# Differential attention written by hand as rows of names: the group norm's matmul placed behind a value or key product, and the first output projection product placed one row earlier where the heads end

## Chip, cores and metric

The program runs on one core of a Trainium2 chip. The metric is the time of one execution in microseconds (us) as the device reports it; of several executions the median counts. A separate execution was recorded by the hardware profiler, and all quoted rows come from it. TensorE is PE in the profile (its weight loads are PEld), VectorE is DVE, ScalarE is ACT, GpSimd is POOL, and SyncE, which issues most DMAs, is SP.

## What is computed

The program is a two-layer encoder trunk on 1024 tokens of width 1024. Layer 0 mixes tokens by differential attention and layer 1 by latent attention; each is followed by a gated MLP with a short convolution. The change touches only layer 0's attention and the start of its output projection:

```python
def block(args):
    qb, blk = args
    sc = jnp.einsum('bqhcd,bkhcd->bhcqk', qb, k).astype(jnp.float32) * scale
    p = masked_softmax(sc, chunk_mask(blk, s)[None, None, None])
    a = p[:, :, 0] - lam * p[:, :, 1]
    return jnp.einsum('bhqk,bkhe->bqhe', a.astype(v.dtype), v)
...
o = from_blocks(lax.map(block, (to_blocks(q), jnp.arange(nb))))
o = rms_norm(o, subln_g) * (1.0 - lambda_init)
return o.reshape(b, s, D_MODEL) @ w_o
```

There are 8 heads, each with two score maps (c = 0 and 1). The softmax of the second, times a scalar, is subtracted from the first; the result weighs the values; each head's output is RMS-normalised over its 128 columns (the group norm) and goes through the output projection.

## The kernel before

Every product of float32 operands is made of three matmuls of high and low parts (`mm3`, lines 119 to 121): high by low, high by high, low by high. So each operand must first be split into a rounded high part (ACT, `hi`, line 127) and the remainder (DVE or POOL, `lo`, line 130).

Attention is cut into 32 steps: step 4h + p is head h with the query pair p, that is 256 query rows against the keys up to there. A step is an object (`DaStep`) with small named parts, and a unit of projection work (queries, keys or values of 512 tokens) has named parts too. `da_steps` (line 346) walks through rows t = -1 to 34. A row is a string of names; a name without a mark belongs to step t, with one `'` to step t - 1, with two to step t - 2, with `+` to step t + 1. Names of steps that don't exist are passed over. The rows are taken from `DA_SCORE[t % 4]`, with `DA_SECOND` for t = 1 and the seven rows of `DA_END` for t = 28 to 34. Within these rows the order on PE, DVE, ACT and POOL is exactly that of the names (`manual_schedule`); SP's DMAs are placed by the framework's own scheduler.

The names that matter here:

- `S0`, `S1` are the scores of the two query blocks (lines 1871 and 1872), `M` their row maxima (DVE, line 1886 or 1882), `E` the exponentials (ACT, line 1897), `I` the reciprocals of the sums, `C` the scaling of the first map, `X0`, `X1` the subtraction of the second map (DVE, line 1910).
- `T` turns a piece of the weights on PE (line 1918), `H` and `L` split it (ACT, DVE), `A` multiplies it by the values on PE, `O` copies the result out (ACT).
- `Q1`, `Q2`, `Q3` square the output for the group norm: two on ACT (lines 1952, 1955), `Q3` on POOL, the remainder (line 130). `F` sums the squares over the columns with two matmuls by ones (lines 1963, 1964). `R1`, `R2`, `R3` on ACT (lines 1970, 1972, 1974) and `N1`, `N2`, `N3` on DVE (1979, 1981, 1983) make the inverse root and store the head's output.
- `U0`, `U1` are the first and second half (12 matmuls each) of a projection product, `V0`, `V1` those of the row's second unit. Both accumulate in the one PSUM bank with the tag `u`. For queries and keys the bank is read out by `Us` and `Um` on DVE (lines 601 and 605); `Ua`, `Up` go on on POOL; `Uqa` to `Uqf` split the queries on ACT and POOL.
- In the last rows `d`, `b`, `c` load and split the output projection's weights (`c3` on DVE), `g0` issues the loads for output tile 0, `h0` (ACT) and `l0` (POOL) split its input, `Y0` and `Z0` are the two halves of its product, 12 matmuls each into the bank `u`, and `y0`, `z0` add them to the residual (DVE, line 746).

PSUM has eight banks: three with the tag `b` (turned pieces, outputs, the norm's sums), one `u`, and two pairs `S`. In rows with p of 2 or 3 each `S0` or `S1` takes both `S` pairs, one for each score map, so `S1` writes where `S0`'s scores were, after `E0a` and `E0b` have read them.

Of the kernel before, what the change touches and what calls it, by code (L numbers as in the profile page):

```python
# [56 lines left out]
class Trunk:  # L57
# [234 lines left out]
    def steps(self, attend, units, prepare, n, apart=False):  # L292
# [33 lines left out]

    DA_SCORE = (
# [4 lines left out]
    )  # L332

    DA_SECOND = "S0 I1' Vc' H2'' M0 Ukd' L2'' A1'' C0' X0' H3'' E0b L3'' U0 E0a A2'' Wh Vt' N3'''' A3'' O'' Wl' Q2'' C1' I0 X1' U1 C0 S1 X0 Us Vh' Q1'' T0' H0' Q3'' Up F'' Um M1 Ua Wl R1'' Vl' E1b V0 E1a L0' I1 A0' Uqa R2'' R3'' Uqd Uqb C1 N1'' Uqe X1 Uqc V1 T1 T0 Uqf H0"

    DA_END = (
# [9 lines left out]
    def da_steps(self, attend, units, prepare, n, extra):  # L346
# [4 lines left out]
        with self.tc.manual_schedule(engines={E.PE, E.DVE, E.Activation, E.Pool}):  # L351
            for t in range(-1, first + len(self.DA_END)):
                while len(steps) < min(n, t + 2):
# [3 lines left out]
                    for name, u in zip("UV", units(x)):  # L357
                        steps[x].parts.update({name + part: f for part, f in u.items()})
                row = self.DA_SECOND if t == 1 else self.DA_SCORE[t % 4] if t < first else self.DA_END[t - first]
                for name in row.split():  # L360
# [1961 lines left out]
```

## Time and profile before

| what | value |
|---|---|
| median of 3 runs | 2386.11 us (2383.92 to 2387.11) |
| span of the profiled execution | 2381.6 us |
| runs' median less that span | 4.5 us |
| PE busy | 2344.1 us, 98% |
| DVE busy | 1931.5 us, 81% |
| ACT busy | 1288.2 us, 54% |
| POOL busy | 613.7 us, 26% |
| first and last of the 16 group norm sums (`F`, line 1963) | start at 92.6 and 496.9 us |

The profiled execution's own time beside its span is not among the three times; the table gives the distance between the span and the median of the runs instead. A row of the timeline has the start in us from the span's start, the duration, the engine, the line in the kernel, the operation, the tiles written and read, the shape, and how many equal ones were merged; in brackets stands how long the engine was idle before it and what ended that. Matmuls overlap in the pipeline: one of 512 columns lasts 0.39 us, but the next starts about 0.23 us later, so distances between starts are what counts. A row of the view of waits has the waiting instruction, the one waited for, the sum in us, how often, and the longest.

### The profile page before, as it was taken

What the parts mean: (1) busy time and instruction counts of PE and PEld (TensorE: products, weight loads), DVE (VectorE), ACT (ScalarE), POOL (GpSimd) and SP (SyncE); (2) the same over time, 40 slices, a digit from 0 to 9 for tenths busy, and PEclk for the clock granted to TensorE, in tenths of its full rate; (3) what the DMA queues carried; (4) which work ended last, traced back from release to release, by engine and by line L of the source; (5) the groups of instructions that cost most, each with busy time, mean ns of one, the idle gap of its engine ahead of it and who ended that gap; (6) DMA issues with size and microseconds to landing.
All of it is one profiled execution on the core that took longest, in us unless ns stands there. A gap on an engine that the chain in (4) does not pass through costs nothing.

```text
span 2381.6 us, 32686 instructions
## 1 busy us (share of the span) xinstructions
PE 2344.1 (98%) x11954; PEld 1994.6 (84%) x11954; DVE 1931.5 (81%) x3185; ACT 1288.2 (54%) x2365; POOL 613.7 (26%) x486
## 2 busy tenths in 40 slices
PE   8999999999999999999999999999999999999998
PEld 7888888888888888888898889988888888887886
DVE  6788888858888888899865888886588888888997
ACT  6777677735444444354444778775354444443544
POOL 4555555324000000000133666673320000000001
PEclk9999999999999999999999999999999999999999
DMA  3111111332222222652222211133322222227502
GB/s 147 41 36 37 49 36 54 115 111 102 94 83 80 80 89 80 230 167 94 82 97 58 72 32 39 41 98 105 117 74 93 80 80 82 87 80 282 177 1 80
DMA packets 95664, 213.39 MB, mean 90 GB/s; under 512 B 8712, under 2 KB 33936, under 8 KB 95504
## 3 DMA queue, kind: packets, MB, share of 16 engines
q1 hardware_dynamic: 86304, 183.51, 23.3%
q10 hardware_dynamic: 9200, 27.80, 3.2%
q8 instruction: 94, 1.54, 0.3%
q14 instruction: 66, 0.54, 0.1%
HBM read 158.85 MB, written 52.43 MB: 89 GB/s over the span
## 4 chain that ended last, share of the span: by engine, by line
PE 86%; DVE 6%; DMA 2%; POOL 2%; issue 2%; ACT 1%; SPq 0%; POOLq 0%; DVEq 0%; ACTq 0%
PE S L119 13%; PE S L121 13%; PE S L120 13%; PE b L119 8%; PE b L121 8%; PE b L120 8%; PE u L119 4%; PE u L121 4%; PE u L120 4%; PE b L263 2%; PE u L2028 2%; PE u L2027 1%; PE S L1872 1%; PE S L1871 1%; PE b L1918 1%
## 5 line engine op out<-in xcount | busy, mean ns | idle before, releaser
L167 POOL TENSOR_TENSOR st<-st,mhalf 128x1 f32<-128x1 f32 x56 | 35.8, 641 | 1294.3 <-DVE st L164 1286.6
L119 PE MATMUL S<-s,u 128*128 128x512 f32 (+1 forms) x800 | 302.4, 378 | 1.9 <-DVE s L130 1.9
L121 PE MATMUL S<-s,u 128*128 128x512 f32 (+1 forms) x800 | 301.6, 377 | 1.5 <-DVE u L130 0.8
L120 PE MATMUL S<-s,u 128*128 128x512 f32 (+1 forms) x800 | 301.3, 377 | 0.0
L127 ACT CAST u<-h 128x512 fp32r<-128x512 f32 (+2 forms) x242 | 145.6, 619 | 275.2 <-DVE h L1026 271.9
L119 PE MATMUL b<-s,u 128*128 128x512 f32 x588 | 231.0, 393 | 1.1 <-DVE u L130 0.4
L121 PE MATMUL b<-s,u 128*128 128x512 f32 x588 | 229.3, 390 | 0.0
L120 PE MATMUL b<-s,u 128*128 128x512 f32 x588 | 229.2, 390 | 0.0
L1083 DVE SCALAR_TENSOR_TENSOR u<-u,conv,u 128x1023 f32<-128x1023 f32 (+1 forms) x176 | 224.8, 1277 | 0.8 <-ACT u L1079 0.7
L149 POOL TENSOR_TENSOR u<-u,st 128x512 f32<-128x512 f32 (+7 forms) x160 | 172.2, 1085 | 168.5 <-DVE st L2013 106.7
L127 ACT CAST s<-u 128x512 fp32r<-128x512 f32 (+3 forms) x229 | 144.4, 664 | 93.7 <-PE u L121 26.4
L119 PEld LDWEIGHTS S<-s,u 128*128 128x128 f32 x800 | 150.5, 188 | 30.1 <-DVE s L130 2.6
L130 DVE TENSOR_TENSOR u<-b,u 128x512 fp32r<-128x512 f32 (+1 forms) x256 | 158.5, 631 | 21.2 <-ACT u L127 19.1
L121 PEld LDWEIGHTS S<-s,u 128*128 128x128 f32 x800 | 150.6, 188 | 29.3 <-DVE u L130 1.0
L120 PEld LDWEIGHTS S<-s,u 128*128 128x128 f32 x800 | 150.6, 188 | 27.3
L127 ACT CAST u<-b 128x512 fp32r<-128x512 f32 (+1 forms) x256 | 134.6, 547 | 71.0 <-PE b L1918 40.8
L119 PE MATMUL u<-s,s 128*128 128x512 f32 (+1 forms) x408 | 162.7, 399 | 1.6 <-DVE s L130 0.9
L121 PE MATMUL u<-s,s 128*128 128x512 f32 (+1 forms) x408 | 158.1, 388 | 0.0
L120 PE MATMUL u<-s,s 128*128 128x512 f32 (+1 forms) x408 | 157.8, 387 | 0.0
L1086 ACT ACTIVATE u<-u 128x1024 f32<-128x1024 f32 x44 | 46.7, 1062 | 187.4 <-DVE u L1083 187.4
L130 DVE TENSOR_TENSOR s<-u,s 128x512 fp32r<-128x512 f32 (+2 forms) x204 | 139.1, 715 | 10.6 <-ACT s L127 10.3
L130 DVE TENSOR_TENSOR u<-h,u 128x512 fp32r<-128x512 f32 x171 | 117.4, 687 | 32.6 <-ACT u L127 31.5
(294 smaller groups left out, 6518.4 us busy)
## 6 DMA issues: line engine op xcount, KB each, us to landing
u<-in_ffn_up SPq DMA_DIRECT2D x88, 512.0 KB, 3.8
g_d<-u ACTq DMA_DIRECT2D x44, 512.0 KB, 2.6
u<-in_ffn_down SPq DMA_DIRECT2D x66, 256.0 KB, 5.2
u<-g_d SPq DMA_DIRECT2D x62, 256.0 KB, 4.2
s<-in_da_wqkv SPq DMA_DIRECT2D x23, 512.0 KB, 3.6
x_d<-u SPq DMA_DIRECT2D x16, 512.0 KB, 2.9
s<-x_d SPq DMA_DIRECT2D x8, 1024.0 KB, 9.9
u<-o_d SPq DMA_DIRECT2D x24, 256.0 KB, 3.1
```

The lines of the kernel that those rows point to most:

```text
L119: mm(out, lh, rl, start=first, stop=False, skip_group_check=onto)
L120: mm(out, lh, rh, start=False, stop=False, skip_group_check=onto)
L121: mm(out, ll, rh, start=False, stop=last, skip_group_check=onto)
L127: self.nc.scalar.copy(out, src)
L130: (eng or self.nc.vector).tensor_sub(out, src, hi.bitcast(F32))
L149: self.nc.gpsimd.tensor_mul(x, x, s.to_broadcast(list(x.shape)))
L167: nc.gpsimd.tensor_tensor(r, s, self.mhalf, ALU.pow)
L263: self.nc.tensor.transpose(ps[:, j * P : (j + 1) * P], probs[t][:, k : k + P], self.ident)
L1083: nc.vector.scalar_tensor_tensor(t[half][:, back:], u[half][:, : S - back], w, t[half][:, back:], ALU.mult, ALU.add)
L1086: nc.scalar.activation(t[0], t[0], AF.Silu)
L1871: nc.tensor.matmul(sc[c][:, b : b + m], ql[c][:, qs], kt[:, c, :m], start=True, stop=False)
L2028: nc.tensor.matmul(o[:, c0:], v, ah, start=False, stop=kb == 2 * p + 1)
```

## The change

Four rows of names are written anew; no part is added or taken away.

In the second row of `DA_SCORE` (rows 5, 9, 13, 17, 21, 25) `F''` stands behind `V0` instead of ahead of `Um`, and `R1''` stands next to `R2''`. The row for t = 1 has the same edit, but there `F''` and `R1''` belong to step -1, which doesn't exist. In `DA_END`, `g0` and `c3` move up within row 29, and `h0`, `l0` and `Y0` come up from row 30 into row 29:

```diff
-        "S0 I1' Vc' H2'' M0 Ukd' L2'' A1'' C0' X0' H3'' E0b L3'' U0 E0a A2'' Wh Vt' N3'''' A3'' O'' Wl' Q2'' C1' I0 X1' U1 C0 S1 X0 Us Vh' Wl Q1'' T0' H0' Q3'' Up F'' Um M1 Ua R1'' Vl' E1b V0 E1a L0' I1 A0' Uqa R2'' R3'' Uqd Uqb C1 N1'' Uqe X1 Uqc V1 T1 T0 Uqf H0",
+        "S0 I1' Vc' H2'' M0 Ukd' L2'' A1'' C0' X0' H3'' E0b L3'' U0 E0a A2'' Wh Vt' N3'''' A3'' O'' Wl' Q2'' C1' I0 X1' U1 C0 S1 X0 Us Vh' Wl Q1'' T0' H0' Q3'' Up Um M1 Ua Vl' E1b V0 F'' E1a L0' I1 A0' Uqa R1'' R2'' R3'' Uqd Uqb C1 N1'' Uqe X1 Uqc V1 T1 T0 Uqf H0",
...
-        "S0 M0 A1'' Up Ukc' b3 E0a L3'' Ua A2'' X0' A3'' Uqa Ukd' Uqc I1 O'' X1' Q1'' Q2'' Q3'' Uqb Uqd T0' H0' Uqf F'' E0b L0' Uqe g0 c3",
-        "S0 h0 M0a I0' l0 C1' C0' R1''' E0a R2''' M0b g1 A0'' Y0 E0b X1' X0' S1 R3''' h1 g2 T0' N1''' O'' y0 M1b N2''' Vt'' H0' T1' E1b Z0 M1a Vh'' E1a L0' z0 H1' l1 Vl'' L1'",
+        "S0 M0 A1'' Up Ukc' b3 E0a L3'' Ua g0 A2'' X0' A3'' Uqa Ukd' Uqc I1 O'' h0 X1' c3 Q1'' Q2'' l0 Q3'' Uqb Uqd T0' Y0 H0' Uqf F'' E0b L0' Uqe",
+        "S0 M0a I0' C1' C0' R1''' E0a R2''' M0b g1 A0'' E0b X1' X0' S1 R3''' h1 g2 T0' N1''' O'' y0 M1b N2''' Vt'' H0' T1' E1b Z0 M1a Vh'' E1a L0' z0 H1' l1 Vl'' L1'",
```

What this does to the order on PE in row 5 (rows 9, 13, 17, 21 and 25 are alike), before: `T0'` turns into `b_1304`, `F''` sums into `b_1313`, and `V0` starts in the bank `u_1329`, followed by `A0'` into `b_1346`.

```order
L1918 MATMUL b_1304<-ident,u_228_1140 128x128
L1918 MATMUL b_1304<-ident,u_234_1159 128x128 x2
L1963 MATMUL b_1313<-h_257_1310,ones 128x512
L1964 MATMUL b_1313<-h_250_1271,ones 128x512
L119 MATMUL u_1329<-s_51_148,s_212_1070 128x512
...
L119 MATMUL b_1346<-u_256_1308,u_213_1074 128x256
```

And with the change, where the names' numbers are others but the parts the same (`u_1323` is `V0`'s bank, `b_1336` the sum, `b_1343` the output):

```order
L1918 MATMUL b_1304<-ident,u_228_1140 128x128
L1918 MATMUL b_1304<-ident,u_234_1159 128x128 x2
L119 MATMUL u_1323<-s_51_148,s_212_1070 128x512
...
L1963 MATMUL b_1336<-h_257_1310,ones 128x512
L1964 MATMUL b_1336<-h_250_1271,ones 128x512
L119 MATMUL b_1343<-u_256_1308,u_213_1074 128x256
```

The two matmuls by ones moved behind `V0`'s twelve matmuls, so that these now stand directly behind the turning.

On ACT in the same row the piece of the difference is this (line 1970 is `R1''`, lines 1972 and 1974 `R2''` and `R3''`, line 1897 `E1b` and `E1a`, the casts to `u` are the query splits):

```order
-L1970 ACTIVATE h_262_1323<-b_1313,eps 128x512
-L1897 ACTIVATE u_264_1327,st_263_1326<-S_1290,st_260_1318 128x512 x2
-L127 CAST u_267_1353<-h_259_1316 64x512
-L1972 ACTIVATE h_261_1322<-h_262_1323 128x512
-L1974 ACTIVATE h_262_1323<-h_261_1322 128x512
-L127 CAST u_267_1353<-h_259_1316 64x512 x3
+L1897 ACTIVATE u_261_1321,st_260_1320<-S_1290,st_259_1315 128x512 x2
+L127 CAST u_265_1350<-h_258_1313 64x512
+L1970 ACTIVATE h_267_1353<-b_1336,eps 128x512
+L1972 ACTIVATE h_266_1352<-h_267_1353 128x512
+L1974 ACTIVATE h_267_1353<-h_266_1352 128x512
+L127 CAST u_265_1350<-h_258_1313 64x512 x3
```

`R1''` moved from ahead of the two exponentials to right ahead of `R2''`; on DVE the order of this row is unchanged.

At the end of the heads, PE in rows 29 and 30 before: `T0'` into `b_4749`, `F''` into `b_4756`, `S0` into `S_4766` and `S_4767`, `A0''` into `b_4797`, `Y0` into `u_4804`, then `S1` into `S_4821` and `S_4822`.

```order
L1918 MATMUL b_4749<-ident,u_861_4596 128x128 x2
L1963 MATMUL b_4756<-h_890_4745,ones 128x512
L1964 MATMUL b_4756<-h_889_4743,ones 128x512
L1871 MATMUL S_4766<-u_809_4316,h_59_156 128x512
...
L119 MATMUL b_4797<-u_892_4753,u_842_4502 128x256
...
L119 MATMUL u_4804<-s_856_4570,u_897_4776 128x512
...
L1871 MATMUL S_4821<-u_809_4316,h_59_156 128x512
```

And with the change (`b_4756` is now the turned piece, `u_4760` is `Y0`, `b_4776` the sum, `S_4782` `S0`'s scores, `b_4810` `A0''`):

```order
L1918 MATMUL b_4756<-ident,u_861_4596 128x128 x2
L119 MATMUL u_4760<-s_856_4570,u_889_4743 128x512
...
L1963 MATMUL b_4776<-h_892_4752,ones 128x512
L1964 MATMUL b_4776<-h_891_4749,ones 128x512
L1871 MATMUL S_4782<-u_809_4316,h_59_156 128x512
...
L119 MATMUL b_4810<-u_895_4773,u_842_4502 128x256
...
L1871 MATMUL S_4821<-u_809_4316,h_59_156 128x512
```

`Y0`'s twelve matmuls left the place between `S0` and `S1` of row 30 and stand ahead of `F''` and `S0`. On ACT `h0` now precedes `Q1''`, on POOL `l0` precedes `Q3''`, and on DVE `c3` precedes `L0'`; the order of SP's DMAs is the same as before.

More of the change, by code (lines that the diff above doesn't have):

```diff
@@ L332 @@
     )
-    DA_SECOND = "S0 I1' Vc' H2'' M0 Ukd' L2'' A1'' C0' X0' H3'' E0b L3'' U0 E0a A2'' Wh Vt' N3'''' A3'' O'' Wl' Q2'' C1' I0 X1' U1 C0 S1 X0 Us Vh' Q1'' T0' H0' Q3'' Up F'' Um M1 Ua Wl R1'' Vl' E1b V0 E1a L0' I1 A0' Uqa R2'' R3'' Uqd Uqb C1 N1'' Uqe X1 Uqc V1 T1 T0 Uqf H0"
+    DA_SECOND = "S0 I1' Vc' H2'' M0 Ukd' L2'' A1'' C0' X0' H3'' E0b L3'' U0 E0a A2'' Wh Vt' N3'''' A3'' O'' Wl' Q2'' C1' I0 X1' U1 C0 S1 X0 Us Vh' Q1'' T0' H0' Q3'' Up Um M1 Ua Wl Vl' E1b V0 F'' E1a L0' I1 A0' Uqa R1'' R2'' R3'' Uqd Uqb C1 N1'' Uqe X1 Uqc V1 T1 T0 Uqf H0"
     DA_END = (
         "O'' d0 Up X1' S1 S0 V0 R2''' Ua R3''' M1 d1 b0 b1 M0 c0 T0' V1 E1b N1''' T2' H0' L0' E1a c1 Uka +S1 d2 Vc E0a N2''' b2 Ukb E0b N3''' T1' +U0 T3' H2' H1' +M1 I1 +U1 I0 c2 +E1b +E1a L2' L1' d3 +Us A0' +Um C1 C0 H3'",
[2 rows of a table removed]
[2 rows of a table added]
         "S0 I1' A0'' h2 C1' I0' A1'' Y1 C0' O'' M0a X1' X0' y1 g3 T0' Q1'' M0b E0a T2' H0' N3'''' T1' H1' E0b L0' I0 l2 C0 Z1 Q2'' L1' z1 H2' h3",
```

## The prediction

> **What bounds the kernel.** I read the page's first part, then the view of waits with PE as the waiting engine over 60 to 760 us, then the timeline of PE at the waits that the change addresses.
>
> ```profile
> span 2381.6 us, 32686 instructions
> PE 2344.1 (98%) x11954; PEld 1994.6 (84%) x11954; DVE 1931.5 (81%) x3185; ACT 1288.2 (54%) x2365; POOL 613.7 (26%) x486
> PE b L1963 <- POOL h L130: 3.1, 7, 0.8
> ```
>
> PE is busy for 98% of the span, so what isn't a wait of PE, or doesn't become one, costs nothing. The change moves no matmul out of the program. It can gain only from idle PE: `F''` (line 1963) waits seven times for `Q3''` on POOL, 3.1 us in all; six of these are rows 5 to 25, the seventh and longest is row 29.
>
> **Part 1: `F''` behind `V0`, six times.** Row 9 stands for all; its PE, DVE and ACT rows:
>
> ```profile
> 167.50 0.49 PE L1918 MATMUL b<-ident,u 128*128 128x128 f32 x3
> 168.37 0.50 PE L1963 MATMUL b<-h,ones 128*128 128x512 f32 x1 [0.38 <-POOL h L130]
> 168.70 0.40 PE L1964 MATMUL b<-h,ones 128*128 128x512 f32 x1
> 168.94 0.39 PE L119 MATMUL u<-s,s 128*128 128x512 f32 x1
> 171.67 0.28 PE L119 MATMUL b<-u,u 128*128 128x256 f32 x1
> 175.13 0.92 PE L1918 MATMUL b<-ident,u 128*128 128x128 f32 x7
> ...
> 167.73 0.68 DVE L605 TENSOR_TENSOR h<-u,s 128x512 f32<-128x512 f32 x1
> 173.13 0.69 DVE L1979 SCALAR_TENSOR_TENSOR h<-b,h 128x512 f32<-128x512 f32 x1 [1.35 <-ACT h L1974]
> 173.74 0.77 DVE L1910 SCALAR_TENSOR_TENSOR u<-u,st 128x512 f32<-128x512 f32 x1
> ...
> 169.20 0.69 ACT L1970 ACTIVATE h<-b,eps 128x512 f32<-128x512 f32 x1 [0.70 <-PE b L1964]
> 171.23 0.61 ACT L127 CAST u<-h 64x512 fp32r<-64x512 f32 x1
> 171.74 0.63 ACT L1972 ACTIVATE h<-h 128x512 f32<-128x512 f32 x1
> 172.40 0.63 ACT L1974 ACTIVATE h<-h 128x512 f32<-128x512 f32 x1
> ```
>
> `T0'`'s three transposes, 0.11 apart, end their issue near 167.8, and `F''` starts at 168.37. What may be won is this hole, about 0.55 us a row (the view shows 0.38, since it counts from the modelled end of the last transpose). But what comes next with the change, `V0`, writes the bank `u`, and `Um` (line 605) still reads that bank until 167.73 + 0.68 = 168.41. Row 1 of the same profile, where there is no `F''` and `V0` already stands behind `T0'`, shows that wait:
>
> ```profile
> 56.64 0.67 DVE L605 TENSOR_TENSOR h<-u,s 128x512 f32<-128x512 f32 x1
> 57.37 0.50 PE L119 MATMUL u<-s,s 128*128 128x512 f32 x1 [0.16 <-DVE h L605]
> ```
>
> `V0` started 0.05 us after `Um`'s end there (56.64 + 0.67 = 57.31). In row 9 it would start at 168.46, 0.09 us later than `F''` does now. So **one wait takes the place of the other**: nothing on DVE ahead of `Um` is moved. The rest is the same work in another order: restart 0.10 (168.70 less 168.37 is 0.33 where pitch is 0.23), twelve matmuls in 171.67 - 168.94 = 2.73, and `F''`'s pair 0.46. `F''` starts at 171.29 and 171.52, `A0'` at 171.75 instead of 171.67: **+0.08 us**.
>
> What is late next is the norm's chain, which now starts 2.8 us later. `R1''` started 0.50 after the second matmul of `F''` (169.20 - 168.70), so it now starts at 172.02, behind the first query split (171.23 + 0.61 = 171.84). Behind it `R2''` and `R3''` follow without a gap: 0.72 for `R1''` and a pitch of 0.66 (172.40 - 171.74) for `R2''` put `R3''` at 173.40, its end at 174.03 instead of 173.03. `N1''` waits for it (the bracket: 1.35 us idle until line 1974) and starts 0.10 after, at 174.13. Queued behind `N1''` on DVE is `X1`: 0.61 later, 174.74, with 0.77 of its own to 175.51. `T1`'s second transpose needs `X1`. `T1` comes up on PE at 175.13 + 0.08 = 175.21, its second transpose at 175.32, and `X1`'s result is there at 175.51 + 0.05 = 175.56. That is a **new stall of 0.24, or 0.30 us with a restart of some 0.06** (an estimate from the 0.10 of the long matmul). Today `X1` ends at 174.51, 0.62 ahead of `T1`: this cover is used up. The three query splits queued behind `R3''` (0.64 each) end near 175.95; the next `S0`, which needs the last of them at its fourth matmul, comes up only behind `T1` and `T0` and their 0.92, near 176.2; nothing there.
>
> A row loses 0.08 + 0.30 = 0.38; six rows **+2.3 us**. Bounds: -0.55 x 6 = -3.3 if neither wait came, +0.5 if only `V0`'s came, and with an `X1` that loses another 0.2 to POOL beside it +3.5. I take the middle of the chain as worked out.
>
> **Part 2: `Y0` ahead of `F''` in row 29.** The rows of before around it:
>
> ```profile
> 445.67 0.44 PE L1918 MATMUL b<-ident,u 128*128 128x128 f32 x2 [1.64 <-DVE u L1910]
> 446.88 0.79 PE L1963 MATMUL b<-h,ones 128*128 128x512 f32 x1 [0.77 <-POOL h L130]
> 447.90 0.63 PE L1871 MATMUL S<-u,h 128*128 128x512 f32 x1
> 450.21 0.34 PE L119 MATMUL b<-u,u 128*128 128x256 f32 x1
> 455.11 0.60 PE L1918 MATMUL b<-ident,u 128*128 128x128 f32 x4
> 459.08 0.39 PE L1871 MATMUL S<-u,h 128*128 128x512 f32 x1
> ...
> 446.00:447.00 1.00, 0.23 (x3) 0.12 (x1) 0.00 (x0) 0.95 (x3) 0.92 (x2) 0.81 0.00 0
> 447.00:448.00 1.00, 1.00 (x3) 0.81 (x4) 0.69 (x2) 0.95 (x4) 1.00 (x1) 0.50 0.00 0
> 450.00:451.00 1.00, 1.00 (x10) 1.00 (x10) 0.75 (x2) 0.00 (x0) 1.00 (x2) 0.98 0.36 105
> ```
>
> In the last three rows (the view by windows) the first seven fields are time and busy engines, and 0.81, 0.50, 0.98 are PE's granted clock. It was halved from 446.6 to 450.0. The eight matmuls of `S0` took 450.21 - 447.90 = 2.31 us in it. At full clock they take 1.3 (four at 0.23, four short ones at 0.1), and the pair of `F''` 0.56 with its restart instead of 447.90 - 446.88 = 1.02. So lost here: 0.93 waiting for `Q3''` (446.88 less 445.95, where the transposes end) and 1.5 in the slow clock, 2.4 together.
>
> With the change `T0'`'s wait of 1.64 for `X1'` stays, since nothing ahead of `X1'` on DVE moves. `h0` stands on ACT behind `O''`, `l0` on POOL behind a query split, `Q3''` behind `l0`:
>
> ```profile
> 443.94 0.37 ACT L1946 COPY h<-b 128x256 f32<-128x256 f32 x1
> 444.06 1.27 POOL L130 TENSOR_TENSOR h<-h,u 64x512 fp32r<-64x512 f32 x1 [0.73 <-ACT u L127]
> 449.39 1.28 POOL L130 TENSOR_TENSOR u<-s,u 128x512 fp32r<-128x512 f32 x1 [1.21 <-DVE s L130]
> 447.78 1.49 DVE L130 TENSOR_TENSOR s<-s,s 128x1024 fp32r<-128x1024 f32 x1
> 438.59 0.38 SPq L677 DMA_DIRECT2D s<-o_d  x1
> ```
>
> `O''` ends at 444.31, so `h0` (0.6) is done by 445.0, ahead of POOL. The load of `g0` was already issued at 438.59, and SP's order is the same, so no DMA is late on this path. The split on POOL takes 1.28 (the third row is `l0`), so `l0` runs 445.41 to 446.69 and `Q3''` from 446.77 to 448.03. PE does `Y0`'s first two matmuls from 445.95, waits at the third until 446.74 (0.3 us), and ends `Y0` at 446.74 + 0.10 + 10 x 0.23 = 449.14. `c3` on DVE (the fourth row, 1.49), now right behind `X1'`, whose end released PE at 445.67, is done by 447.1, ahead of the tenth matmul, which needs it. `F''` takes 0.46 and waits for nothing. `S0` starts at 449.60 at full clock, takes 1.3, and ends at 450.90, **0.69 later than before**.
>
> Now the place that `Y0` left. `S1` needs both `S` pairs back, through `M0a`, `E0a`, `M0b`, `E0b`:
>
> ```profile
> 450.36 0.82 DVE L1886 TENSOR_REDUCE st<-S 128x1 f32<-128x640 f32 x1
> 451.66 0.82 DVE L1886 TENSOR_REDUCE st<-S 128x1 f32<-128x640 f32 x1
> 452.59 0.78 ACT L1897 ACTIVATE u<-S,st 128x640 f32<-128x640 f32 x1
> 454.62 0.68 DVE L746 TENSOR_TENSOR s<-s,u 128x512 f32<-128x512 f32 x1
> 458.26 0.90 ACT L1897 ACTIVATE u<-S,st 128x768 f32<-128x768 f32 x1 [0.30 <-DVE st L1886]
> ```
>
> From `S0`'s end to `E0b`'s end there are 453.37 - 450.21 = 3.16 us, today covered by `A0''` and `Y0`. Without `Y0`, PE has only `A0''` (six short matmuls, about 0.55) and then waits: `E0a`, as long as `E0b`, follows `M0a` (451.18) and ends near 452.1, with the 0.69 near 452.8, so PE idles 1.3 us before `S1` and 0.8 more before its second score map. `E0b` ends at 453.37 + 0.69 = 454.06, the remaining six matmuls (0.9 and a restart) end `S1` near 455.05, as now (455.11). Up to here it is a draw: the dead time has only moved. But the chain goes on: `N1'''`, `y0`, `M1b`, `M1a`, `E1a` follow each other on DVE and ACT, all 0.69 late. `E1a` (the last row) gave its scores free at about 459.1, and `S0` of row 31, which writes where `E1a` reads, started at 459.08, so there is no slack: it starts at about 459.8. **Part 2: +0.7 us.** Bounds: -2.4 if both the wait and the slow clock went and `S1` came on time; upward +0.7 and the clock's risk on top, below.
>
> **Sum.** 2.3 + 0.7 = +3.0 us, against the span 2381.6: 2384.6. The median of the runs lies 4.5 above the span; I carry that over: **2389.1 us**. About 0.2% (4.8 us) is what a measurement of this kernel can tell from no change, so this is "no difference".
>
> **The clock.** The halved clock began after PE had idled for 1.6 and 0.9 us within 3.4, and lasted 3.4 us. In the changed rows the densest idling in a stretch of 3.4 us is about 1.95 (1.64 and 0.3, at 444 to 447) and 2.1 (at 451.4 to 454): less than the 2.2 or so of before, not much less. Each time the clock drops, 3.4 us of dense matmuls at half speed cost 1.7. The Trainium skill's page "TensorE: Matmul & The Clock Gate" has the window of about 3.4 us and says it runs freely (Part 1), with which the trace agrees (3.4 us from 446.6 to 450.0); its practical rule is that PE must not idle for over about 3.4 us (HAM oscillation). By that rule no drop could come here, and the sum stays +3.0; but by it the drop of before, with no idle longer than 1.64 us, wouldn't have come either, so the row decides.
>
> **The rivals.**
> 1. *The clock drops in the rearranged rows, slower.* Place: rows 29 and 30; price 1.7 us a time; it decides where 3.4 us hold some 2 us of idle PE. One drop gives 2390.8, two 2392.5. For it: the drop of before. Against: the idling is more spread. 0.22.
> 2. *`V0` waits for `Um`, but `T1` isn't late* (`R1''` starts earlier than I count, or `X1` is shorter): 6 x 0.08 + 0.7 = +1.2, 2387.3. Against: the bracket at `N1''` shows DVE waiting for that very chain. 0.13.
> 3. *The change does what its order suggests*: both waits go and nothing is late: -3.3 - 2.4 = -5.7, 2380.4. Against: row 1's wait for line 605. 0.06.
> 4. *It does nothing that counts*: the holes refill exactly, 2386.1. 0.04.
>
> **How the numbers follow.** The forecast has 0.55, the rivals 0.45. The runs of before spread over 3.2 us, so a case's time is good to about 1.5. The range reaches from 2384.6 (rivals 4 and 2 with that spread) to 2393.0 (two drops). Faster by over 0.2% would be below 2381.3: rival 3, 0.05. Slower by over 0.2% is above 2390.9: most of rival 1 and the forecast's upper tail, 0.19. The rest, 0.76, is no difference.
>
> **What would show it.** Right: in rows 5 to 25 no wait of line 1963, but line 119 into `u` waiting for line 605, and line 1918 waiting for DVE line 1910 about 0.2 us each; in row 30 line 1871 waiting for ACT line 1897 twice, and again at row 31. Wrong: `T1` with no idle before it, `S1` without a wait, or waits of line 1871 on the query splits.

## The result, and the profile after

| | before | after |
|---|---|---|
| median of 6 runs each | 2385.0 us (2383.92 to 2387.11) | 2392.4 us (2390.47 to 2394.18) |
| ratio, with its 95% interval | | 1.0029 (1.0019 to 1.0039) |
| span of the profiled execution | 2381.6 us | 2390.9 us |

The changed kernel is 7.4 us slower by the medians. That is inside the range of the prediction, but above its 2389.1 and above the 0.2% within which it had called the result no difference. Of the 9.3 us between the two spans, 0.77 were there before the first `F` (92.63 and 93.40 us), where nothing was changed, and 7.5 lie between the first and the last `F` (404.28 us before, 411.79 now), where all of the change is.

The page's first lines of the changed kernel: the same matmuls, PE busy 4.7 us longer.

```profile
span 2390.9 us, 32680 instructions
PE 2348.8 (98%) x11954; PEld 1994.9 (83%) x11954; DVE 1932.4 (81%) x3185; ACT 1289.1 (54%) x2365; POOL 615.7 (26%) x486
```

The view of waits of the changed kernel, PE as the waiting engine, 60 to 560 us:

```profile
PE b L1918 <- DVE u L1910: 4.8, 2, 4.1
PE u L119 <- DVE h L605: 3.0, 6, 0.5
PE S L1871 <- ACT u L1897: 1.7, 2, 1.2
```

No row of line 1963 is left. In its place stands `V0` waiting for `Um`, six times and about as long (3.0 us); `S1` waits twice for the exponentials; and the longest wait of line 1918 for `X1'`, which had been 1.6 us, is now 4.1. (The other one of line 1918, 0.71 us at 65.4, lies ahead of row 5 and was 0.70 before.)

**Rows 5 to 25.** PE and DVE in row 9 of the changed kernel, and the next `F''` of this kind, four rows on:

```profile
168.61 0.49 PE L1918 MATMUL b<-ident,u 128*128 128x128 f32 x3
169.59 0.50 PE L119 MATMUL u<-s,s 128*128 128x512 f32 x1 [0.50 <-DVE h L605]
172.45 0.40 PE L1963 MATMUL b<-h,ones 128*128 128x512 f32 x1
176.37 1.13 PE L1918 MATMUL b<-ident,u 128*128 128x128 f32 x7
228.06 0.40 PE L1963 MATMUL b<-h,ones 128*128 128x512 f32 x1
...
168.87 0.67 DVE L605 TENSOR_TENSOR h<-u,s 128x512 f32<-128x512 f32 x1
175.22 0.69 DVE L1979 SCALAR_TENSOR_TENSOR h<-b,h 128x512 f32<-128x512 f32 x1 [2.31 <-ACT h L1974]
175.83 0.74 DVE L1910 SCALAR_TENSOR_TENSOR u<-u,st 128x512 f32<-128x512 f32 x1
```

And the same `F''` four rows on in the kernel before:

```profile
223.59 0.50 PE L1963 MATMUL b<-h,ones 128*128 128x512 f32 x1 [0.38 <-POOL h L130]
```

Four rows took 223.59 - 168.37 = 55.22 us before and take 228.06 - 172.45 = 55.61 now: +0.39. From `T0'` to `T1` it is 7.76 instead of 7.63 us, and the seven transposes of `T1` and `T0` last 1.13 instead of 0.92, because `X1` (175.83 + 0.74 = 176.57) ends 0.2 us after `T1` has begun. In all six rows the second transpose starts 0.26 us behind the first instead of 0.11. The view of waits counts from the modelled end of the first, so it doesn't show this stall.

**Rows 29 to 31.** PE, then DVE, then POOL of the changed kernel (line 1910 at 447.64 is `X1'`; the four rows of line 130 on POOL are a query split, `l0`, `Q3''` and the next query split):

```profile
451.21 0.69 PE L1918 MATMUL b<-ident,u 128*128 128x128 f32 x2 [4.09 <-DVE u L1910]
451.56 0.78 PE L119 MATMUL u<-s,u 128*128 128x512 f32 x1
456.82 0.42 PE L1963 MATMUL b<-h,ones 128*128 128x512 f32 x1
460.64 0.50 PE L1871 MATMUL S<-u,h 128*128 128x512 f32 x1 [1.17 <-ACT u L1897]
461.94 0.50 PE L1871 MATMUL S<-u,h 128*128 128x512 f32 x1 [0.56 <-ACT u L1897]
462.98 0.60 PE L1918 MATMUL b<-ident,u 128*128 128x128 f32 x4
466.95 0.39 PE L1871 MATMUL S<-u,h 128*128 128x512 f32 x1
467.68 0.50 PE L1871 MATMUL S<-u,h 128*128 128x512 f32 x1
...
447.64 3.52 DVE L1910 SCALAR_TENSOR_TENSOR u<-u,st 128x256 f32<-128x256 f32 x1
...
447.16 1.27 POOL L130 TENSOR_TENSOR h<-h,u 64x512 fp32r<-64x512 f32 x1 [0.73 <-ACT u L127]
448.39 1.26 POOL L130 TENSOR_TENSOR u<-s,u 128x512 fp32r<-128x512 f32 x1
449.62 1.25 POOL L130 TENSOR_TENSOR h<-h,h 128x512 fp32r<-128x512 f32 x1
450.95 1.33 POOL L130 TENSOR_TENSOR h<-h,u 64x512 fp32r<-64x512 f32 x1
```

`X1'` lasts 3.52 us. The kernel before has the same operation on the same shape:

```profile
444.55 1.07 DVE L1910 SCALAR_TENSOR_TENSOR u<-u,st 128x256 f32<-128x256 f32 x1
...
445.57 1.26 POOL L130 TENSOR_TENSOR h<-h,h 128x512 fp32r<-128x512 f32 x1 [0.24 <-ACT h L1955]
```

There POOL paused for 0.24 us ahead of `Q3''`, and `X1'` ended 0.29 us behind the start of that pause (445.62, with the query split ahead of it ending at 444.06 + 1.27 = 445.33). In the changed kernel `l0` fills the pause: each POOL row begins where the one ahead of it ends, up to a pause of 0.08 us at 449.62 + 1.25 = 450.87, and `X1'` again ends 0.29 us behind the start of the pause.

The view by windows of the changed kernel (time, then PE, PE's loads, DVE, ACT and POOL busy, then PE's granted clock) shows what the longer wait does next:

```profile
448.00:450.00 2.00, 0.00 (x0) 0.00 (x0) 2.00 (x1) 1.95 (x4) 2.00 (x3) 1.00 0.10 39
450.00:452.00 2.00, 0.79 (x3) 0.79 (x4) 2.00 (x2) 0.31 (x2) 1.92 (x2) 0.51 0.00 0
452.00:454.00 2.00, 2.00 (x6) 1.52 (x6) 1.84 (x2) 1.71 (x4) 1.92 (x2) 0.50 0.00 0
454.00:456.00 2.00, 2.00 (x7) 1.52 (x6) 0.00 (x0) 0.00 (x0) 0.27 (x1) 0.50 0.64 190
456.00:458.00 2.00, 2.00 (x8) 1.60 (x7) 0.00 (x0) 0.42 (x1) 0.00 (x0) 0.78 0.24 72
```

The clock is halved from about 450 to 457, so all of `Y0` ran at half speed: from 451.56 to `F''` at 456.82 are 5.26 us for twelve matmuls that take 12 x 0.23 + 0.1 = 2.86 at full clock. From `T0'`'s second transpose to `S0` of row 31 it is 466.95 - 451.21 = 15.74 us, where it was 459.08 - 445.67 = 13.41: +2.33, and the wait of `T0'` ahead of that is 2.45 longer. Together +4.8 us in this one place, in this one execution.

### The profile page after: what moved, and what is told of

It reads as the page before. It is cut to its first block, busy times and chain, and to the rows that moved or that the text cites. A ratio compares the mean times of both kernels' runs of the same rounds, so it can differ in the third digit from the quotient of the medians.

```text
span 2390.9 us, 32680 instructions
## 1 busy us (share of the span) xinstructions
PE 2348.8 (98%) x11954; PEld 1994.9 (83%) x11954; DVE 1932.4 (81%) x3185; ACT 1289.1 (54%) x2365; POOL 615.7 (26%) x486
## 4 chain that ended last, share of the span: by engine, by line
PE 86%; DVE 8%; DMA 2%; issue 2%; ACT 1%; POOL 1%; SPq 0%; DVEq 0%; POOLq 0%; ACTq 0%
PE S L119 13%; PE S L121 13%; PE S L120 13%; PE b L119 8%; PE b L120 8%; PE b L121 8%; PE u L119 4%; PE u L121 4%; PE u L120 4%; PE b L263 2%; PE u L2028 1%; PE u L2027 1%; PE S L1871 1%; PE S L1872 1%; PE b L1918 1%
```

## The experiments

All times are medians with the ratio to the kernel before, run on the same chip beside it. Row names are as in the change.

**1 and 2. The two halves of the change alone.** The first kernel has the new score rows and the old end rows, the second the reverse:

```diff
-        ... Q3'' Up F'' Um M1 Ua R1'' Vl' E1b V0 E1a ...
+        ... Q3'' Up Um M1 Ua Vl' E1b V0 F'' E1a ...
```

```diff
-        ... I1 O'' X1' Q1'' Q2'' Q3'' Uqb Uqd T0' H0' Uqf F'' ... g0 c3",
-        "S0 h0 M0a I0' l0 C1' ... A0'' Y0 E0b ...",
+        ... I1 O'' h0 X1' c3 Q1'' Q2'' l0 Q3'' Uqb Uqd T0' Y0 H0' Uqf F'' ...",
+        "S0 M0a I0' C1' ... A0'' E0b ...",
```

> The new score rows alone (F'' behind V0), the end rows as before. Theory A (the prediction's two waits cost 0.38 us a row): +2.3 us against before, ratio about 1.0010, 6 waits of line 119 on line 605 of about 0.5 us each, and 6 stalls of T1's second transpose of about 0.2 us. Rival (these rows are neutral and all of the loss is at the end): within 0.5 us of before, ratio 1.000.

Measured: 2387.04 against 2384.81 us, ratio 1.0012 (1.0003 to 1.0020). Four rows take 55.62 us, and row 29 is as before (`X1'` 1.07, `T0'` waiting 1.65 us). So the score rows alone cost 2.2 us, and none of it comes from the end rows.

> The new end rows alone, the score rows as before. Theory P (in row 29 X1' on DVE is held up while POOL runs the query split, l0 and Q3'' without a gap): X1' lasts 3.5 us instead of 1.1, T0' waits 4.1 us instead of 1.6, the clock is halved for two stretches of 3.4 us, +5 us against before, ratio about 1.002. Rival (the two edits disturb each other, for instance through the time at which a DMA lands): X1' near 1.1 us and less than +2 us here.

Measured: 2389.21 against 2384.81 us, ratio 1.0019 (1.0010 to 1.0028): +4.4 us. `X1'` on DVE, for which `T0'` waits 4.09 us here too:

```profile
444.93 3.51 DVE L1910 SCALAR_TENSOR_TENSOR u<-u,st 128x256 f32<-128x256 f32 x1
```

The long `X1'` belongs to the end rows, whatever the score rows do. The halves add up within their intervals: 2.2 + 4.4 = 6.6 against 7.4.

**3. The splits moved up, `Y0` left in row 30.**

```diff
-        ... Uqd T0' Y0 H0' Uqf F'' ...
+        ... Uqd T0' H0' Uqf F'' ...
-        "S0 M0a I0' C1' C0' R1''' E0a R2''' M0b g1 A0'' E0b ...
+        "S0 M0a I0' C1' C0' R1''' E0a R2''' M0b g1 A0'' Y0 E0b ...
```

> The new row 29 without Y0, which stays between S0 and S1 of row 30; g0, h0, l0 and c3 are moved up as in the change. Theory P: l0 on POOL ahead of Q3'' is what matters, so X1' lasts 3.5 us again and T0' waits 4.1 us, though Y0 has not moved; F'' then waits for nothing, S1 waits for nothing, +1.5 to +3.5 us. Rival (X1' is late because of what Y0 does on PE, or because of c3 behind it): X1' near 1.1 us, T0' waits 1.6 us, and F'' waits some 2 us for Q3'', which l0 has put back: about +1.3 us.

Measured: 2385.58 against 2384.81 us, ratio 1.0004 (0.9995 to 1.0013): +0.8 by the medians, less than expected. The stage in the table further down is 2.1 us longer, but in that execution the clock was halved for longer than in the one before. `X1'` takes 3.51 and `T0'` waits 4.09 us here too, without `Y0`; `S1` waits for nothing:

```profile
PE b L1918 <- DVE u L1910: 4.1, 1, 4.1
PE b L119 <- DVE u L130: 0.3, 1, 0.3
```

So `Y0` isn't what makes `X1'` long, and `S1`'s waits come from `Y0`'s leaving row 30. A part of the long wait is paid back where `F''` no longer waits for `Q3''`.

**4. The new end rows, but `l0` on DVE behind `X1'`.**

```diff
-            put(f"l{n}", lambda st: self.lo(st.ol, st.o, st.oh, nc.gpsimd), st)
+            put(f"l{n}", lambda st, eng: self.lo(st.ol, st.o, st.oh, eng), st, nc.vector if n == 0 else nc.gpsimd)
...
-        ... h0 X1' c3 Q1'' Q2'' l0 Q3'' ...
+        ... h0 X1' l0 c3 Q1'' Q2'' Q3'' ...
```

> The new end rows with l0 done on DVE right behind X1' instead of on POOL, the rest of the end rows as in the change, the score rows as before. Theory P: without l0 POOL has a gap ahead of Q3'', X1' lasts 1.1 us, T0' waits 1.6 us; Y0's third matmul waits less than 0.6 us, S1 still waits twice, about 2 us together, for the exponentials: +0.5 to +2.5 us against before. Rival (X1' is held by the DMA traffic or by h0 on ACT): X1' lasts 3.5 us again, +5 us.

Measured: 2385.96 against 2384.81 us, ratio 1.0006 (0.9997 to 1.0015). DVE, PE, and two windows:

```profile
444.84 1.07 DVE L1910 SCALAR_TENSOR_TENSOR u<-u,st 128x256 f32<-128x256 f32 x1
...
445.97 0.44 PE L1918 MATMUL b<-ident,u 128*128 128x128 f32 x2 [1.65 <-DVE u L1910]
453.42 0.50 PE L1871 MATMUL S<-u,h 128*128 128x512 f32 x1 [1.18 <-ACT u L1897]
...
448.00:450.00 2.00, 1.69 (x8) 1.08 (x7) 1.21 (x2) 1.37 (x4) 1.92 (x2) 1.00 0.42 127
456.00:458.00 2.00, 2.00 (x11) 2.00 (x11) 1.59 (x4) 0.32 (x1) 1.05 (x1) 0.50 0.00 0
```

With one operation less on POOL, `X1'` is back at 1.07 and `T0'` at 1.65 us, and `Y0` runs at full clock (1.00 in the first window). `S1`'s waits stay, and behind them the clock drops for one stretch. But for this drop, and for a wait of 0.31 us of `Y0`'s tenth matmul for `c3`, which takes 2.31 us here, this is what the prediction had described for Part 2.

**5. The new score rows, with `X1` ahead of `N1''` on DVE.**

```diff
-        ... Uqb C1 N1'' Uqe X1 Uqc V1 T1 T0 ...
+        ... Uqb C1 X1 Uqe N1'' Uqc V1 T1 T0 ...
```

> The new score rows with the old end rows (as in the run with the score rows alone, +2.2 us), and on DVE X1 placed ahead of N1'' instead of behind it. If the prediction's chain is right (X1 is late only because it is queued behind N1'', which waits for R3'' on ACT), then the idle time of DVE ahead of N1'' is used for X1, T1's second transpose (line 1918 behind DVE line 1910) waits no more, and what is left of Part 1 is V0's wait for Um and the restart, some 0.08 us a row: the period of four rows falls from 55.63 back to about 55.30, and the program takes 0.5 us more than before (ratio 1.0002), not 2.2. Rival: X1 is held by the work of POOL beside it (C1, then the query splits), wherever it stands; then T1 still waits 0.2 us or more and the time stays at +2.2 us or above.

Measured: 2386.09 against 2385.21 us, ratio 1.0002 (0.9993 to 1.0011). DVE and PE in row 9:

```profile
173.52 1.77 DVE L1910 SCALAR_TENSOR_TENSOR u<-u,st 128x512 f32<-128x512 f32 x1 [0.97 <-POOL u L149]
175.22 0.68 DVE L1979 SCALAR_TENSOR_TENSOR h<-b,h 128x512 f32<-128x512 f32 x1
...
172.08 0.40 PE L1963 MATMUL b<-h,ones 128*128 128x512 f32 x1
176.01 0.93 PE L1918 MATMUL b<-ident,u 128*128 128x128 f32 x7
227.42 0.40 PE L1963 MATMUL b<-h,ones 128*128 128x512 f32 x1
```

Four rows take 55.34 us, +0.12 instead of +0.39, and `T1` and `T0` last 0.93 us again. The queue behind `N1''` was the cause of `T1`'s stall. `X1` takes 1.77 us instead of 0.74, with a query split on POOL beside it, but ends in time. The clock of this execution was halved for longer at the end than in the kernel before (see the table).

**6 and 7. `Wl` (a split of 128x1024 on POOL) behind `C1'` instead of behind `Vh'`,** in the rows of before, and in the new score rows with the old end rows. In the kernel before `X1'` and `X0` (one merged row of DVE) took 3.77 us, `X0` beside `Wl`. The first line is theirs, the second that of `Wl`:

```profile
163.41 3.77 DVE L1910 SCALAR_TENSOR_TENSOR u<-u,st 128x256 f32<-128x256 f32 x2
...
164.17 2.59 POOL L130 TENSOR_TENSOR s<-s,s 128x1024 fp32r<-128x1024 f32 x1
```

```diff
-        ... Wl' Q2'' C1' I0 X1' U1 C0 S1 X0 Us Vh' Wl Q1'' ...
+        ... Wl' Q2'' C1' Wl I0 X1' U1 C0 S1 X0 Us Vh' Q1'' ...
```

> All rows of before, but in the second row of the score rows (rows 5 to 25) Wl, a split of 128x1024 on POOL of 2.6 us, stands directly behind C1' instead of behind Vh', so that it runs in POOL's idle time ahead of C0 instead of beside X0. If an operation of DVE with two inputs in SBUF is held while POOL works (the reading of the end rows: X1' 1.07 us alone, 3.5 us beside POOL), X0 falls from 2.75 to about 0.7 us, Um and Q3'' come earlier by some 0.5 us or more, line 1963 waits no longer for POOL in these rows, and the period of four rows falls by the hole of 0.55 from 55.21 to about 54.7: 3.3 us faster than before (ratio 0.9986). Rival: X0 takes 2.75 us for a reason of its own (its length of 384 columns, a wait inside it); then it still takes 2.75 us and the time stays within 0.5 us of before, or worse by what C0 is now late behind Wl.

Measured: 2388.47 against 2385.21 us, ratio 1.0012 (1.0003 to 1.0021): slower by 3.3 us where faster by 3.3 was expected. DVE and PE of the sixth kernel:

```profile
163.28 2.71 DVE L1983 SCALAR_TENSOR_TENSOR h<-h,g_sub,h 128x512 f32<-128x512 f32 x1
166.22 1.62 DVE L1910 SCALAR_TENSOR_TENSOR u<-u,st 128x256 f32<-128x256 f32 x2
...
169.72 0.50 PE L1963 MATMUL b<-h,ones 128*128 128x512 f32 x1 [0.93 <-POOL h L130]
```

`X1'` and `X0` take 1.62 us together now: `X1'` as long as before (1.09 and 1.08 us, beside the same POOL operation of line 149), `X0` 0.61 instead of 2.75. So it was `X0` that `Wl` held. But `N3''''` (line 1983, 0.74 us in row 9 of before) now falls beside `Wl` and takes 2.71. The store behind it comes late, `Q3''` waits for that store by the trace, and `F''` waits 0.93 us here instead of 0.38. The mechanism was right, the place was worse.

> The new score rows with the old end rows, and Wl moved as in the run before. If the X0 held by Wl is what makes Um late, V0 no longer waits for Um (line 119 behind line 605), which the prediction took as the wait that replaces the one removed; what is left is T1's wait for X1, whose chain hangs on F'' behind V0: it comes up to 0.5 us earlier together with all of PE's work, so that T1 still waits some 0.2 us. Expected: the period of four rows at 54.9 to 55.1, the program 1 to 2 us faster than before and 1 to 2 us slower than with Wl moved alone. Rival: X0 is not held by Wl; then +2.2 us as with the new score rows alone.

Measured: 2387.47 against 2385.21 us, ratio 1.0009 (1.0001 to 1.0018), where a gain was expected. `V0`'s wait for `Um` fell from 0.5 to 0.3 us and no further: `N3''''` takes 2.67 us here too, so `X1'` and `X0`, though short together, come late, and `Us` and `Um` behind them. Line 1918 waits for `X1` as well: by the view of waits 3.6 us in all, but 1.6 of them in row 29 and 0.7 ahead of row 5, both as before.

**8. The splits moved up, `Y0` in row 30, and `l0` behind `Q3''` on POOL.**

```diff
-        ... c3 Q1'' Q2'' l0 Q3'' Uqb ...
+        ... c3 Q1'' Q2'' Q3'' l0 Uqb ...
```

> As the run with the splits h0 and l0 in row 29 and Y0 back in row 30 (X1' 3.51 us, T0' waiting 4.09 us), but with l0 behind Q3'' on POOL instead of ahead of it. The same operations run on POOL in row 29. In the trace of before POOL stands idle ahead of Q3'', which waits for Q2'' on ACT. Theory: X1' is let in where POOL pauses, and is shut out as long as POOL's instructions follow each other without a pause. Then X1' goes back to about 1.07 us, T0' to a wait of 1.65 us, F'' to one of some 0.8 to 0.9 us, and the time stands at that of before (ratio 0.9996 to 1.0004). Rival: X1' pays for the amount of POOL's work in the row, l0's 1.26 us above all; then it stays at 2.3 us or more and T0' waits 2.9 us or more.

Measured: 2387.29 against 2385.26 us, ratio 1.0010 (1.0001 to 1.0019). DVE, POOL and PE:

```profile
445.21 1.06 DVE L1910 SCALAR_TENSOR_TENSOR u<-u,st 128x256 f32<-128x256 f32 x1
446.20 1.21 DVE L130 TENSOR_TENSOR s<-s,s 128x1024 fp32r<-128x1024 f32 x1
...
446.61 1.93 POOL L130 TENSOR_TENSOR h<-h,h 128x512 fp32r<-128x512 f32 x1 [0.62 <-ACT h L1955]
...
448.59 0.80 PE L1963 MATMUL b<-h,ones 128*128 128x512 f32 x1 [1.77 <-POOL h L130]
451.18 0.79 PE L1871 MATMUL S<-u,h 128*128 128x512 f32 x1 [0.51 <-POOL h L130]
```

POOL has the same work in the row as in the third run, but it pauses for 0.62 us ahead of `Q3''`, and `X1'` takes 1.06 instead of 3.51 us. So the pause decides, not the amount. The time was expected to stand at that of before and is 2.0 us above it: `c3` on DVE now runs first and `Q3''` on POOL is held beside it (1.93 us instead of 1.26), so `F''` waits 1.77. So the blocking goes both ways. `S0` waits another 0.51 us for the query split that `l0` has put back, and the clock was halved in this execution for 10.2 us.

**9 and 10. `Wl` still earlier,** directly behind `Wl'`, and in the tenth behind `C1'`, with its high part `Wh` moved up into idle time of ACT:

```diff
-        ... H2'' M0 ... A2'' Wh Vt' ... Wl' Q2'' C1' I0 X1' ... Us Vh' Wl Q1'' ...
+        ... H2'' Wh M0 ... A2'' Vt' ... Wl' Wl Q2'' C1' I0 X1' ... Us Vh' Q1'' ...
```

> All rows of before, but in the second row of the score rows Wh stands on ACT directly behind H2'' (where ACT is idle for 1.4 us) and Wl on POOL directly behind Wl', so that POOL's big split runs before N3'''', X1' and X0 on DVE instead of beside one of them. In the run with Wl behind C1' the split held N3'''' (2.71 us for 0.74), C0 and X0 came late, and the program took 3.3 us more. Theory: with Wl done by about the start of N3'''', N3'''' takes some 0.7 to 0.9 us, X0 takes 0.6 to 0.8 us, Q3'' comes at least 0.55 us earlier against PE's work, line 1963 waits no longer for POOL in these rows, and the period of four rows falls from 55.21 to about 54.7: 3 us faster than before (ratio 0.9987). Rival 1: POOL's two big splits in one piece hold Ukd' or X0' (DVE, between) until both are done, and what follows on DVE is late by 1 us or more: then the time is at that of before or above. Rival 2: Wh, earlier on ACT, waits for its weights or its buffer and delays the exponentials: PE waits at the scores, slower.

Measured: 2390.75 against 2385.26 us, ratio 1.0024 (1.0015 to 1.0033). DVE, POOL and PE of the ninth kernel (line 614 is `Ukd'`):

```profile
162.12 2.89 DVE L614 SCALAR_TENSOR_TENSOR u<-h,u 64x512 fp32r<-64x512 f32 x1
...
159.71 4.75 POOL L130 TENSOR_TENSOR s<-s,s 128x1024 fp32r<-128x1024 f32 x2
...
165.79 0.39 PE L119 MATMUL b<-u,u 128*128 128x256 f32 x1 [1.49 <-DVE u L130]
```

Slower by 5.5 us, where faster by 3 was expected. `F''` waits no longer in these rows, but `Ukd'` is held until `Wl` is done, and behind it on DVE stands `L2''`, for which PE waits 1.49 us: the first rival.

> As the run before, with Wl one place later on POOL, behind C1' instead of ahead of it: Wl then runs from about 160.6 to 163.0 of row 9, and X0' and N3'''' on DVE fall into it. By the theory that an operation of DVE with two inputs in SBUF is shut out while POOL works, X0' or N3'''' is held until 163.0 at most, some 1 us less than with Wl behind C1' and Wh in its old place; X0 at 0.6 to 0.8 us, line 1963 with a wait of 0 to 0.3 us a row, the time 1 to 3 us faster than before (ratio 0.9987 to 0.9996). Rival: what is held once holds everything behind it on DVE, and Q3'' or Um come as late as before: within 0.5 us of before, or slower.

Measured: 2390.24 against 2385.26 us, ratio 1.0021 (1.0012 to 1.0030). Here `X0'`, an operation of 128 columns, takes 1.76 us instead of 0.34; PE waits 0.71 us for the split behind it, and `F''` still waits 0.25. Slower by 5.0 us, where faster by 1 to 3 was expected: the rival again. Nothing that was run is faster than the kernel before; every place tried for `Wl` put another operation of DVE beside it.

The end rows side by side. The stage runs from `T0'`'s first transpose in row 29, ahead of the wait, to `S0` of row 31. The clock is the mean that PE was granted from 443 to 463 us; 0.91 means halved for 3.4 us in all, 0.83 for 6.8, and 0.74 for 10.2:

| kernel | `X1'` | `T0'` waits | `S1` waits | clock | stage | ratio |
|---|---|---|---|---|---|---|
| before | 1.07 | 1.64 | none | 0.91 | 15.35 | 1 |
| 1, these rows as before | 1.07 | 1.65 | none | 0.91 | 15.58 | 1.0012 |
| 5, these rows as before | 1.07 | 1.65 | none | 0.83 | 17.52 | 1.0002 |
| the change | 3.52 | 4.09 | 1.17, 0.56 | 0.83 | 20.12 | 1.0029 |
| 2, end rows alone | 3.51 | 4.09 | 1.17, 0.57 | 0.83 | 20.74 | 1.0019 |
| 3, without `Y0` | 3.51 | 4.09 | none | 0.83 | 17.44 | 1.0004 |
| 4, `l0` on DVE | 1.07 | 1.65 | 1.18, 0.56 | 0.91 | 17.24 | 1.0006 |
| 8, `l0` behind `Q3''` | 1.06 | 1.65 | none | 0.74 | 19.21 | 1.0010 |

The first and the fifth kernel have the end rows of before, with the same waits ahead of `S0`, and yet their stages differ by 1.9 us, since the clock of one execution was halved for twice as long. So `X1'` and the waits are what these rows cause, but a stage from a single profile holds some 2 us of the clock's chance, and the ratios, from 11 executions or (the change) 6, count for the time.

## Why the prediction was right or wrong

**Part 1 was right, in mechanism and size.** It gave +0.38 us a row and +2.3 in all; the trace shows +0.39 a row, and the first run 2.2 us for these rows alone. `V0`'s wait for `Um` came at every one of the six rows. `T1`'s stall came from where the prediction put it, since the fifth run takes it away by putting `X1` ahead of `N1''`. The split between the two terms was a little off: 0.13 instead of 0.08 up to `T1`, and the rest behind it.

**Part 2 was wrong in one step above all.** The prediction wrote: "With the change `T0'`'s wait of 1.64 for `X1'` stays, since nothing ahead of `X1'` on DVE moves." It looked for a cause in DVE's own queue and for a semaphore. For an `X1` beside POOL it had allowed 0.2 us in Part 1, for `X1'` in Part 2 nothing. But `X1'` reads both of its inputs from SBUF, and such an operation didn't get on while POOL worked without a pause. `l0`, moved in front of `Q3''`, closed the pause. (The prediction had counted 0.08 us between POOL's operations there, 445.33 to 445.41 and 446.69 to 446.77; the changed kernel has such a pause only behind `Q3''`.) The wait grew by 2.45 us. The fourth and the eighth run take the pause's loss back in two ways, and each brings `X1'` to 1.07 us or less.

The sign of it was in the trace of before: there `X1'` and `X0` took 3.77 us, with `X0` beside `Wl`, and the sixth run shows 1.62 without it. The prediction read the group of line 1910 for its waits and not for durations that differ at one shape.

The Trainium skill's page "SBUF — State Buffer", section "SBUF: two separate sides", states the rule that spoke against this: an operation of DVE with two inputs in SBUF and a GpSimd instruction that reads SBUF exclude each other, and whichever starts first has the shared ports for its whole instruction. The runs agree for the single instruction (`X0` behind `Wl`, `Q3''` behind `c3`). That DVE can be passed over two times running, as `X1'` was by `l0` and by `Q3''`, the page doesn't state.

**The clock's rival came true, out of the wrong cause.** Its two drops were priced at 2392.5 in all, near the 2392.4 measured, and they set the upper end of the range, but that the time lies there is partly luck. PE's idle time was not the 1.95 us in 3.4 of the prediction but 4.09 in one piece, and the halved clock fell on all of `Y0`; by the table, how long the clock stays halved also differs at equal waits. The terms of rows 29 to 31, from the prediction's +0.7: the longer wait +2.45, `Y0` at half speed 5.26 - 2.86 = +2.4, `l0` no longer late for `Y0` -0.3, from `F''` to the end of `S1` 462.98 - 456.82 = 6.16 us where the prediction had 455.05 - 449.14 = 5.91, +0.25, and `S0` of row 31 in time, -0.7. That makes 4.8, as in the trace up to `S0` of row 31.

**`S1`'s two waits were right, the wait behind them was not.** 1.3 and 0.8 us were given; 1.17 and 0.56 came in the change, and nearly the same in the second and in the fourth run, and none where `Y0` stayed in row 30. But the +0.7 itself was to come from `S0` of row 31, which was to wait for `E1a`. `S0` started in time (466.95), while `E1a` still ran (466.63 + 0.90 = 467.53), and only its third matmul was late, by 0.27 us (467.68 instead of 466.95 + 2 x 0.23 = 467.41).

**"No difference" was wrong,** by the step above. Without the held `X1'`, Parts 1 and 2 would make 2.2 + 1.1 (first and fourth run) = 3.3 us, near the +3.0 of the forecast; these are the medians of two separate runs, each good to about 2 us, and no run has both.

## What to carry to other kernels

Before an operation is moved on POOL, look at which operations of DVE with two inputs in SBUF run beside it, and who waits for those: a pause of POOL can be what lets them through, though no semaphore says so. Durations that differ at one shape in the trace of before are the place to find this. And where work that covers a wait is moved away, price the wait it uncovers: that part of the prediction held in every run. Where the clock of TensorE drops, read a stage of a single profile with the granted clock beside it, and compare kernels by many executions.

## What the runs showed of the hardware that was not expected

- An operation of DVE of 128x256 that takes 1.07 us beside one POOL instruction took 3.51 to 3.52 us beside three that followed each other without a pause, in three kernels; it ended 0.28 to 0.29 us behind the third, as it does behind the one (445.62 and 445.33). Elsewhere DVE was let in at such a seam: behind `Wl` in the kernel before, `X0` ended at 163.41 + 3.77 = 167.18, when `Q3''` had been running since 166.72; `Q3''` lasted 1.60 us there instead of 1.26. What decides at a seam who comes first was not found.
- Operations of DVE with an input in PSUM showed nothing of this: a split of 128x384 from PSUM took 0.55 us beside a POOL instruction (at 445.48 and 453.29 of the changed kernel), and 0.55 with POOL idle (at 161.96 of the kernel before).
- In the fourth run the granted clock fell behind two waits of PE of 1.18 and 0.56 us (0.50 at 456 to 458), so it doesn't take one of 4.09. By the rule of the Trainium skill's page "TensorE: Matmul & The Clock Gate" (HAM oscillation), no idle time over about 3.4 us, there would have been no drop in that run; the measured clock decides. In the profiles of seven kernels with the end rows of before, PE waits 1.63 to 1.65 and then 0.77 to 0.79 us in row 29; the clock was halved there for 3.4 us in five of them and for 6.8 in two (the fifth and the ninth run). What exactly sets it off, and how long it lasts, stays open.
